# Layer 0 without GpSimd's wide elementwise work, and 24 modulation rows as float32 products on four 32-column strips

## The chip, the cores and the metric

One core of one Trainium2 chip runs the kernel. The metric is the device time of one execution in microseconds (us). The engines are TensorE (PE; its weight loads are shown as PEld), VectorE (DVE), ScalarE (ACT), GpSimd (POOL) and SyncE (SP), which issues the loads.

## The reference

A trunk of two layers over 256 tokens of width 1024, everything in float32. Each layer is a mixer and a gated ConvFFN, each behind an RMSNorm whose scale, shift and gate come from a conditioning vector `c`:

```python
c_act = jax.nn.silu(c)
for layer in range(DEPTH):
    mod = c_act @ ada_w[layer] + ada_b[layer]          # 1024 x 6144 weights
    sh1, sc1, g1, sh2, sc2, g2 = jnp.split(mod, 6, axis=-1)
    hmix = rmsnorm(x, norm_mix[layer]) * (1.0 + sc1) + sh1
    y = hgrn2_mixer(hmix, ...) if layer == 0 else nsa_mixer(hmix, ...)
    x = x + g1 * y
    hffn = rmsnorm(x, norm_ffn[layer]) * (1.0 + sc2) + sh2
    x = x + g2 * conv_ffn(hffn, ...)
return rmsnorm(x, final_norm)
```

HGRN2, the mixer of layer 0, is a gated linear recurrence with 8 heads of 128. It projects `hmix` to queries q, forget gates f, inputs i and output gates g, runs the recurrence, norms each head, multiplies by silu(g) and projects back to the width of the trunk.

## The kernel before, in words

Activations lie feature-major: 8 chunks of 128 features on the partitions, 256 tokens along the row. A matrix product is made of three float32r products: both the weights and the activations are split into a high and a low part (`whi`, `wlo`, `XH`, `XL`), and high x high, high x low and low x high are added up in PSUM (`mm3`).

All weights come through one stream (class `Stream`). A unit is 128 x 1024 values (512 KB), loaded by SP into one of seven `raw` buffers. A unit of weights is then split: ACT casts `whi` (L106), and DVE, or in some units POOL, subtracts it to get `wlo` (L113), into one of five split buffers. `use(k)` is called where TensorE takes unit k. It splits ahead up to unit k + 3, so whatever a split issues stands in program order ahead of the products of unit k. SP and PE run in the order of the program; DVE, ACT and POOL are ordered by Tile's priorities, except in the opening, which is written out by hand.

Among the units of weights lie 96 rows of the modulation (function `ada`): a unit holds 128 features of one row, one per partition, and one DVE instruction multiplies it by silu(c), broadcast to all partitions in `cb`, and sums along the row into a column of `mod` (L244). In layer 0 some rows go another way: POOL multiplies (L241), and ACT sums in a second pass over the row (L242).

Layer 0 has these stages, by the profile's clock:

- **The opening** (to about 75 us, `opening`): eight chunks of the normed residual, each with two rows of the modulation (the even one on POOL) and two units of weights, `hg_a`. DVE's order per chunk is: row, the columns `gs_t` and `sh_t` of the next chunk, `xn`, `XL`, `wlo`, (row,) `wlo`. PE's order per chunk is eight products each of (`XH`, `whi`), (`XL`, `whi`), (`XH`, `wlo`) at L379, then twelve 512 wide ones at L484. In chunks 2 to 5 the second `wlo` is halved between DVE and POOL (`U1`).
- **Preparing the first four heads** (to about 87 us): `prepare` makes queries, gates and keys; POOL scales the keys (L575) and subtracts three whole units (`HG_LOW`); PE starts the token-major products `hg_i2`.
- **The first chain** (to about 134 us): `diag`, five `level`s and three `blocks`, each a group of float32 products into a PSUM bank of the tag `aux` (which has two banks). After each, `grow` multiplies the queries `hqp` on DVE (L617) and the keys `hks` on POOL (L618). Between the steps of the chain PE does products of `hg_b` (`weave`).
- **The values of the first heads and the second chain** (to about 185 us): the same for heads 4 to 7, with products of `hg_g2` in between.
- **The tail of the mixer** (to about 209 us): values and turn of the second heads, the projection `hg_out`, and the residual (`finish_out`); then `ffn` begins with `mod_cols` and the norm.

From the third unit of `hg_b` to the last of `hg_out`, 18 units of weights have 24 rows among them (`mix`): 8 gates of the mixer and the 16 shift and scale rows of the ConvFFN. Before, every second of the 24 goes to POOL and ACT, the others to DVE.

## Time and profile before

| | us |
|---|---|
| median of 3 runs | 777.64 (776.15 to 781.36) |
| span of the profiled execution, first to last instruction | 774.9 |
| busy in that span: PE / DVE / ACT / POOL | 725.1 / 598.5 / 410.4 / 230.6 |
| mean granted clock of TensorE | 0.968 |
| loaded from memory | 158.48 MB, 206 GB/s over the span |

The profile gives no time of its own execution beside the span; the median lies 2.7 us above the span. A busy share is an average over stages with different limits, and a PE that shows as busy can still run at half clock or be held up by its weight loads. So stages have to be read one by one.

### The profile page before, as it was taken

The page shows a single profiled execution, that of the slowest core. Times are in us where ns is not written, and L with a number is a line of the kernel's source. Part 1 is how long each engine was busy: PE and PEld are TensorE (multiplying, and loading weights), DVE is VectorE, ACT ScalarE, POOL GpSimd, SP SyncE. Part 2 cuts the span into 40 slices and gives each one's busy share as a digit, 9 for nine tenths or more (in the row PEclk, how much of TensorE's full clock was granted, in tenths as well). Part 3 has the DMA queues.
Part 4 walks back from the last instruction along what each step waited for, and adds up shares of the span by engine and source line. Part 5 has one row for each costly group of instructions (what it writes and reads, how often), then busy time and mean ns, then how long its engine had stood idle before and what let it go on. Part 6 is the DMA issues. An engine that isn't in the chain of part 4 may idle for free.

```text
span 774.9 us, 14443 instructions
## 1 busy us (share of the span) xinstructions
PE 725.1 (94%) x5492; PEld 678.1 (88%) x5492; DVE 598.5 (77%) x1041; ACT 410.4 (53%) x756; POOL 230.6 (30%) x247
## 2 busy tenths in 40 slices
PE   7879888888999999999999999999999999999996
PEld 6767778768999999999989987756889999999995
DVE  5999987898599788778969877886768866666653
ACT  4456325426366444446545676776545744555544
POOL 4455647564203135111130015543520201101102
PEclk8999989999999999999999999987999999999998
DMA  8789655755368888899957960010237666776701
GB/s 302 269 274 313 204 191 191 268 192 193 110 219 300 297 280 270 294 267 341 344 191 254 355 207 21 35 56 1 85 134 271 196 217 214 215 221 210 209 18 55
DMA packets 48855, 160.45 MB, mean 207 GB/s; under 512 B 9362, under 2 KB 9618, under 8 KB 48787
## 3 DMA queue, kind: packets, MB, share of 16 engines
q1 hardware_dynamic: 48496, 159.02, 61.8%
q8 instruction: 43, 0.70, 0.4%
q10 hardware_dynamic: 290, 0.53, 0.2%
q14 instruction: 26, 0.20, 0.1%
HBM read 158.48 MB, written 1.05 MB: 206 GB/s over the span
## 4 chain that ended last, share of the span: by engine, by line
PE 72%; DVE 14%; issue 5%; POOL 5%; ACT 3%; DMA 2%; POOLq 0%; DVEq 0%; ACTq 0%
PE mm L316 10%; PE mm L318 10%; PE mm L317 10%; PE acc L379 9%; PE acc L317 7%; PE acc L316 7%; PE acc L318 7%; DVE wlo L113 4%; DVE raw L244 4%; PE acc L1006 2%; PE aux L1076 2%; PE aux L599 2%; POOL wlo L113 1%; PE acc L1005 1%; DMA raw<-ada 1%
## 5 line engine op out<-in xcount | busy, mean ns | idle before, releaser
L113 DVE TENSOR_TENSOR wlo<-raw,whi 128x1024 fp32r<-128x1024 f32 x193 | 247.1, 1291 | 66.8 <-ACT whi L106 66.5
L106 ACT CAST whi<-raw 128x1024 fp32r<-128x1024 f32 x201 | 207.9, 1047 | 138.2 <-PE acc L317 56.3
L316 PE MATMUL mm<-XH,whi 128*128 128x256 f32 x640 | 180.8, 283 | 1.0 <-DVE ff L791 0.9
L318 PE MATMUL mm<-XH,wlo 128*128 128x256 f32 x640 | 178.7, 279 | 0.0
L317 PE MATMUL mm<-XL,whi 128*128 128x256 f32 x640 | 178.4, 279 | 0.0
L796 POOL TENSOR_TENSOR fl<-ff,fh 128x256 fp32r<-128x256 f32 x44 | 43.9, 1002 | 302.9 <-ACT fh L794 297.8
L244 DVE SCALAR_TENSOR_TENSOR raw<-raw,cb 128x1024 f32<-128x1024 f32 x77 | 107.1, 1392 | 25.3 <-DMA raw<-ada 25.2
L316 PEld LDWEIGHTS mm<-XH,whi 128*128 128x128 f32 x640 | 119.9, 187 | 3.9 <-DVE ff L791 1.4
L318 PEld LDWEIGHTS mm<-XH,wlo 128*128 128x128 f32 x640 | 120.2, 188 | 0.0
L317 PEld LDWEIGHTS mm<-XL,whi 128*128 128x128 f32 x640 | 120.1, 188 | 0.0
L317 PE MATMUL acc<-fl,whi 128*128 128x256 f32 x352 | 98.5, 280 | 0.3 <-POOL fl L796 0.3
L316 PE MATMUL acc<-fh,whi 128*128 128x256 f32 x352 | 98.5, 280 | 0.0
L318 PE MATMUL acc<-fh,wlo 128*128 128x256 f32 x352 | 98.4, 280 | 0.0
L317 PEld LDWEIGHTS acc<-fl,whi 128*128 128x128 f32 x352 | 66.2, 188 | 0.5 <-POOL fl L796 0.5
L318 PEld LDWEIGHTS acc<-fh,wlo 128*128 128x128 f32 x352 | 66.2, 188 | 0.0
L316 PEld LDWEIGHTS acc<-fh,whi 128*128 128x128 f32 x352 | 66.1, 188 | 0.0
L241 POOL TENSOR_TENSOR raw<-raw,cb 128x1024 f32<-128x1024 f32 x19 | 49.4, 2599 | 14.2 <-DVE sh_t L414 9.2
L113 POOL TENSOR_TENSOR wlo<-raw,whi 128x1024 fp32r<-128x1024 f32 (+1 forms) x12 | 30.7, 2558 | 69.4 <-ACT whi L106 69.4
L379 PE MATMUL acc<-XH,whi 128*128 128x256 f32 x256 | 36.2, 283 | 8.8 <-ACT XH L398 8.0
L789 ACT ACTIVATE cv<-cv 128x256 f32<-128x256 f32 x44 | 18.0, 415 | 46.8 <-DVE cv L788 46.5
L379 PEld LDWEIGHTS acc<-XH,whi 128*128 128x128 f32 x256 | 32.5, 188 | 11.6 <-ACT XH L398 10.3
L1028 POOL TENSOR_SCALAR PR<-PR,rsum 128x128 f32<-128x128 f32 (+1 forms) x64 | 28.3, 463 | 43.3 <-DVE SC L1015 24.0
(221 smaller groups left out, 1456.4 us busy)
## 6 DMA issues: line engine op xcount, KB each, us to landing
raw<-ada SPq DMA_DIRECT2D x96, 512.0 KB, 4.9
raw<-up SPq DMA_DIRECT2D x88, 512.0 KB, 4.6
raw<-down SPq DMA_DIRECT2D x44, 512.0 KB, 4.5
raw<-hg_a SPq DMA_DIRECT2D x16, 512.0 KB, 5.9
raw<-hg_b SPq DMA_DIRECT2D x8, 512.0 KB, 5.8
raw<-hg_out SPq DMA_DIRECT2D x8, 512.0 KB, 4.5
raw<-nsa_a SPq DMA_DIRECT2D x8, 512.0 KB, 4.8
raw<-nsa_q SPq DMA_DIRECT2D x8, 512.0 KB, 4.9
```

The source lines that it names most:

```text
L106: self.nc.scalar.copy(hi, t)
L113: eng.tensor_sub(lo[:, c], t[:, c], hi[:, c].bitcast(FT))
L241: nc.gpsimd.tensor_mul(t, t, cb)
L244: nc.vector.scalar_tensor_tensor(t, t, 1.0, cb, op0=OP.mult, op1=OP.mult, accum_out=m)
L316: nc.tensor.matmul(o, wh, xh, start=start, stop=False, skip_group_check=True)
L317: nc.tensor.matmul(o, wh, xl, start=False, stop=False, skip_group_check=True)
L318: nc.tensor.matmul(o, wl, xh, start=False, stop=stop, skip_group_check=True)
L379: nc.tensor.matmul(half(accs, m), a[:, w], x[:, c], start=c == 0 and m % 2 == 0 and n == 0, stop=c == NC - 1 and n == 2, skip_group_check= ...
L599: nc.tensor.matmul(ps[:, (2 * h + t) * 64:(2 * h + t + 1) * 64], self.KS[:, h, x], q, start=True, stop=True)
L789: nc.scalar.activation(t, t, AF.Silu)
L796: return nc.gpsimd.tensor_sub(fl, f, fh.bitcast(FT))
L1028: nc.gpsimd.tensor_scalar(p, p, r[:, t, br:br + 1], 0.0, op0=OP.mult, op1=OP.add)
```

## The change

Seven rows of the opening, four halved `wlo` and three whole `wlo` move from POOL to DVE. The scaling of the keys (8 instructions) and their growth (28) move from POOL to DVE. What POOL keeps in layer 0 is small: the `pow` of the norms, the adds of squares and some fills.

The 24 rows between the third unit of `hg_b` and the end of `hg_out` are no longer sums on DVE, POOL and ACT. Their weights come transposed (`ada_k`), again 24 units of 512 KB: a pair of units holds two rows' 2 x 128 features as columns, and 8 chunks of the contraction, four per unit. When the second unit of a pair is split, PE multiplies all eight chunks in float32: the stationary operand is a chunk of silu(c), repeated over 32 columns (`cs`), the moving one 256 columns of weights. The four chunks of a unit go to four strips of 32 output partitions, and the second unit adds to the same strips. ACT copies the 128 x 256 result to SBUF (`sums`); one step of the stream later (`turned`) PE adds up the four strips and turns them onto the partitions with two products against a column `quarter`, and DVE copies two columns to `mod`. `mix` gives the unit of the first row of a pair the first half and that of the second the other, so the rows' places in the stream stay. The last pair is turned at the start of `ffn`, ahead of `mod_cols`. Silu of `c` for `cs` is computed in the opening ahead of the squares of the norm.

```diff
@@ -106,11 +104,7 @@
         def rest():
-            parts = low if isinstance(low, tuple) else (low,)
-            w = D // len(parts)
-            for n, eng in enumerate(parts):
-                c = slice(n * w, (n + 1) * w)
-                eng.tensor_sub(lo[:, c], t[:, c], hi[:, c].bitcast(FT))
+            low.tensor_sub(lo, t, hi.bitcast(FT))
...
@@ -223,6 +217,12 @@
+    ccol = consts.tile([P, NC], FT, name="ccol")
+    cs = consts.tile([P, NC, 32], FT, name="cs")
+    quarter = consts.tile([P, 1], FT, name="quarter")
+    nc.gpsimd.memset(quarter, 0.0)
+    for j in range(4):
+        nc.gpsimd.memset(quarter[32 * j:32 * j + 1], 1.0)
...
+    held, turning = [], []
+
+    def turned():
+        while turning:
+            turning.pop(0)()
+
+    def ada_pair(n, half):
+        def then(t):
+            held.append(t)
+            if not half:
+                return turned()
+            tiles = [held.pop(0) for _ in range(2)]
+            turned()
+            ps = bank("aux")
+            for u, x in enumerate(tiles):
+                for j in range(4):
+                    nc.tensor.matmul(ps[32 * j:32 * j + 32, :S], cs[:, 4 * u + j], x[:, j * S:(j + 1) * S],
+                                     start=u == 0, stop=u == 1, skip_group_check=True)
+            sums = work.tile([P, S], FT, name="sums")
+            nc.scalar.copy(sums, ps[:, :S])
+
+            def turn():
+                for k in range(2):
+                    nc.tensor.matmul(ps[:, S + k:S + k + 1], sums[:, k * P:(k + 1) * P], quarter, start=True, stop=True,
+                                     skip_group_check=True)
+                nc.vector.tensor_copy(mod[:, n:n + 2], ps[:, S:S + 2])
+
+            turning.append(turn)
+        return st.add(I["ada_k"][:, (n - 16) // 2, half], then)
...
@@ -270,13 +301,13 @@
         if c + 1 < NC:
-            ada(2 * c + 2, pool=True)
-        u_a[c].append(st.add(I["hg_a"][:, c, 1], low=(nc.vector, nc.gpsimd) if c in U1 else None))
+            ada(2 * c + 2)
+        u_a[c].append(st.add(I["hg_a"][:, c, 1]))
...
-    ids = mix(ws[:HG_LATE], [], low=HG_LOW) + mix(ws[HG_LATE:], ada_units(0, "g1") + ada_units(0, "2"), range(0, 24, HG_POOL))
+    ids = mix(ws[:HG_LATE], []) + mix(ws[HG_LATE:], ada_units(0, "g1") + ada_units(0, "2"), pairs_=True)
...
@@ -517,6 +548,8 @@
         lower_bound()
+        nc.scalar.activation(ccol, part("c"), AF.Silu)
+        nc.vector.tensor_copy(cs, ccol[:, :, None].to_broadcast([P, NC, 32]))
         norm = Norm(7, nc.vector)
...
@@ -572,7 +605,7 @@
-                nc.gpsimd.tensor_scalar(self.KS[:, h], self.KS[:, h], a, 0.0, op0=OP.mult, op1=OP.add)
+                nc.vector.tensor_scalar(self.KS[:, h], self.KS[:, h], a, None, op0=OP.mult)
...
@@ -615,7 +648,7 @@
-                    nc.gpsimd.tensor_mul(k[:, hs], k[:, hs], T[:, hs, :, 1:2].to_broadcast([P, 2, n // 2, m]))
+                    nc.vector.tensor_mul(k[:, hs], k[:, hs], T[:, hs, :, 1:2].to_broadcast([P, 2, n // 2, m]))
...
@@ -759,6 +792,7 @@
     weave((critical(B.chain()), HG_WEAVE[0]), (one_after_another(first_of(g2, HG_TURN), A.turn(), g2, *outs[:HG_OUT[0]]), HG_WEAVE[1]))
+    turned()
     gate_cols(0)
...
         first, units = u_f[layer]
+        turned()
         mod_cols(k, nffn, 0, NC)
```

## Rows read from the trace of the kernel before

**Rows 1.** Windows: stages of layer 0; length, busy us per engine (instructions), PE clock, DMA, GB/s

```profile
47.80:55.80 8.00, 5.89 (x36) 4.99 (x36) 7.41 (x8) 3.42 (x6) 4.59 (x2) 1.00 0.81 256
63.80:69.60 5.80, 5.76 (x37) 5.20 (x38) 5.16 (x10) 3.99 (x6) 0.00 (x0) 1.00 0.82 270
...
87.20:134.20 47.00, 40.14 (x327) 38.92 (x328) 37.43 (x56) 16.59 (x26) 28.73 (x21) 0.89 0.60 201
134.20:184.85 50.65, 42.46 (x282) 36.74 (x281) 46.26 (x70) 22.68 (x51) 30.52 (x23) 0.90 0.63 212
184.85:208.90 24.05, 24.05 (x206) 24.05 (x205) 15.62 (x30) 12.44 (x32) 5.46 (x7) 1.00 0.56 190
```

**Rows 2.** Timeline, chunk 4 of the opening: start, length, engine, line, tiles [idle before]

```profile
48.21 2.93 DVE L113 TENSOR_TENSOR wlo<-raw,whi 128x1024 fp32r<-128x1024 f32 x2
...
50.55 2.84 POOL L241 TENSOR_TENSOR raw<-raw,cb 128x1024 f32<-128x1024 f32 x1
...
51.06 3.41 DVE L244 SCALAR_TENSOR_TENSOR raw<-raw,cb 128x1024 f32<-128x1024 f32 x1
```

**Rows 3.** Timeline, chunk 1 of the opening, where POOL has nothing to do

```profile
22.52 1.21 DVE L244 SCALAR_TENSOR_TENSOR raw<-raw,cb 128x1024 f32<-128x1024 f32 x1
...
25.49 2.35 DVE L113 TENSOR_TENSOR wlo<-raw,whi 128x1024 fp32r<-128x1024 f32 x2
...
27.76 1.22 DVE L244 SCALAR_TENSOR_TENSOR raw<-raw,cb 128x1024 f32<-128x1024 f32 x1
```

**Rows 4.** Timeline, first products of chunks 1, 4 and 7

```profile
25.36 1.10 PE L379 MATMUL acc<-XH,whi 128*128 128x256 f32 x8
...
47.83 1.21 PE L379 MATMUL acc<-XH,whi 128*128 128x256 f32 x8 [2.24 <-ACT XH L398]
...
69.58 1.10 PE L379 MATMUL acc<-XH,whi 128*128 128x256 f32 x8
```

**Rows 5.** Timeline, from the opening to the first chain

```profile
75.54 0.47 PE L316 MATMUL mm<-whi,XH 128*128 128x512 f32 x1 [0.17 <-DVE V L742]
...
76.03 5.79 POOL L113 TENSOR_TENSOR wlo<-raw,whi 128x1024 fp32r<-128x1024 f32 x2
...
81.85 1.95 PE L585 MATMUL aux<-hq,hks 128*128 128x128 f32 x16
...
87.20 0.39 PE L318 MATMUL acc<-XH,wlo 128*128 128x256 f32 x1 [3.16 <-DVE wlo L113]
```

**Rows 6.** Groups by line and shape, 18 to 209 us: xcount | busy us, mean ns

```profile
L617 DVE TENSOR_TENSOR hqp<-hqp,ht 128x256 f32<-128x256 f32 x28 | 25.8, 947 | 2.3 <-PE aux L599 1.9 <-PE aux L641 0.3
...
L618 POOL TENSOR_TENSOR hks<-hks,ht 128x256 f32<-128x256 f32 x28 | 26.8, 970 | 35.5 <-PE aux L599 25.8 <-issue 5.2 <-DVE OL L701 1.8
```

**Rows 7.** Timeline, levels of both chains: DVE with nothing of POOL's in the way

```profile
104.77 0.77 DVE L605 COPY_PREDICATED hst<-masks,aux 128x256 f32<-128x256 uint32 x2
...
161.33 0.78 DVE L617 TENSOR_TENSOR hqp<-hqp,ht 128x256 f32<-128x256 f32 x2
```

**Rows 8.** Timeline, float32 products, each two passes; and the product behind the third

```profile
7.06 1.98 PE L516 MATMUL mm<-cb,ones 1*128 1x512 f32 x4
...
119.61 0.70 PE L630 MATMUL aux<-hqp,hks 128*32 128x32 f32 x32
120.24 0.39 PE L316 MATMUL acc<-XH,whi 128*128 128x256 f32 x1
...
134.19 1.05 PE L669 MATMUL aux<-V,hst 128*128 128x128 f32 x8
```

**Rows 9.** Windows: the clock around the first two of these (columns as in rows 1)

```profile
7.06:9.00 1.94, 1.94 (x6) 0.69 (x5) 1.33 (x4) 1.75 (x4) 0.00 (x0) 1.00 1.00 357
...
119.60:120.20 0.60, 0.60 (x33) 0.59 (x32) 0.60 (x2) 0.60 (x1) 0.60 (x2) 1.00 0.75 239
```

**Rows 10.** Waits of PE, 75 to 209 us: us in total, times, longest

```profile
PE aux L599 <- DVE hqp L617: 6.6, 5, 2.3
```

**Rows 11.** Timeline, DVE where the ConvFFN's norm begins

```profile
210.65 0.16 DVE L325 TENSOR_SCALAR msq<-aux 128x2 f32<-128x2 f32 x1 [1.43 <-PE aux L361]
```

More of the change, by code (lines that the diff above doesn't have):

```diff
@@ L39 @@
 TSOON = 75
-U1 = range(2, 6)
 HG_LATE = 6
 FFN_LATE = 8
-HG_POOL = 2
-HG_LOW = (0, 1, 2)
 NSA_LOW = (6, 8)
@@ L62 @@
 SMALL = {}
-for _n, _w in (("ada_b", 96), ("norm_mix", 16), ("norm_ffn", 16), ("final_norm", 8), ("hg_lb", 16), ("hg_gnorm", 1)):
+for _n, _w in (("ada_b", 96), ("norm_mix", 16), ("norm_ffn", 16), ("final_norm", 8), ("hg_lb", 16), ("hg_gnorm", 1),
+               ("c", 8)):
     SMALL[_n] = (sum(w for _, w in SMALL.values()), _w)
@@ L234, in trunk, with ada @@
     st = Stream(nc, raws, splits, *LOOK)
-    def ada(n, pool=False):
+    def ada(n):
         def then(t):
-            m = mod[:, n:n + 1]
-            if pool:
-                nc.gpsimd.tensor_mul(t, t, cb)
-                return lambda: nc.scalar.activation(t, t, AF.Copy, accum_out=m)
-            else:
-                nc.vector.scalar_tensor_tensor(t, t, 1.0, cb, op0=OP.mult, op1=OP.mult, accum_out=m)
-        return st.add(I["ada"][:, n], then)
+            nc.vector.scalar_tensor_tensor(t, t, 1.0, cb, op0=OP.mult, op1=OP.mult, accum_out=mod[:, n:n + 1])
+        return st.add(I["ada"][:, n], then)
+    held, turning = [], []
[23 more added lines that the diff above has]
+        return st.add(I["ada_k"][:, (n - 16) // 2, half], then)
     def ada_units(layer, which):
@@ L251, in ada_units, with mix @@
         return list(range(b + a, b + e))
-    def mix(ws, adas_, pool=(), low=()):
+    def mix(ws, adas_, low=(), pairs_=False):
         ids, n, m = [], len(ws), len(adas_)
@@ L259, in mix @@
             while done < m and done * n < (k + 1) * m:
-                ada(adas_[done], done in pool)
+                if pairs_:
+                    ada_pair(adas_[done - done % 2], done % 2)
+                else:
+                    ada(adas_[done])
                 done += 1
@@ L1183, in _layout @@
     a["ada"] = order(f["ada_w"].transpose(0, 2, 1))
-    small = {"ada_b": order(f["ada_b"])}
+    a["ada_k"] = a["ada"][:, 16:40].reshape(P, 12, 2, 2, 4, P).transpose(5, 1, 3, 4, 2, 0).reshape(P, 12, 2, D)
+    small = {"ada_b": order(f["ada_b"]), "c": f["c"].reshape(NC, P).T}
     for n in ("norm_mix", "norm_ffn"):
```

## The prediction

> **What bounds the kernel now.** I read the page first (PE busy in 94% of the span), then windows by stage, because only layer 0 is touched. Behind it, from 209 us on, nothing of the change runs, so the whole difference must arise ahead of it. The windows [rows 1] show three kinds of stage. In a chunk of the opening PE is busy 5.89 of 8.00 us while DVE shows 7.41 and POOL 4.59. In the two chains PE shows 40.14 of 47.00 and 42.46 of 50.65, but at a mean clock of 0.89 and 0.90: there PE waits, cools down and then works at half speed. In the tail of the mixer PE is busy 24.05 of 24.05 us at full clock: nothing is idle there.
>
> Next the timeline of a chunk [rows 2], to see why DVE is so full. A row of the modulation takes 1.21 us on DVE where POOL has nothing to do [rows 3], but 3.41 beside POOL's product of 2.84, and ends right with it (50.55 + 2.84 = 53.39; 51.06 + 3.41 = 54.47, one undisturbed row behind). Two `wlo` take 2.35 undisturbed [rows 3] and 2.93 beside POOL [rows 2]. So DVE does not share with POOL, it stands still. The same shows in the chains: L617 takes 0.39 alone [rows 7] and 0.95 in the mean [rows 6]. Every microsecond of POOL's wide work costs DVE nearly one. The waits of PE then name DVE: 6.6 us on `hqp` alone [rows 10], and 3.16 at the end of the preparation, where POOL's two `wlo` of 5.79 had held up DVE [rows 5].
>
> The Trainium skill, SBUF — State Buffer, section "SBUF: two separate sides", calls the ports that these two engines share an exclusive lock. The trace agrees (1.21 against 3.41).
>
> **The change part by part.**
>
> *Opening, chunks 1 to 7.* Undisturbed, the period with one row on DVE is 27.76 - 22.52 = 5.24 us [rows 3]. The second row adds 1.21 and its accumulator read, so I take 6.5 for chunks 1 to 6; the halved `wlo` is already whole in that period. The last period is undisturbed today and stays 5.8 [rows 1]. From chunk 1 to 7: 5 x 6.5 + 5.8 = 38.3 against 69.58 - 25.36 = 44.2 [rows 4], **-6**. DVE is still the bound (PE needs 5.89 [rows 1]). The loads must bring 2.1 MB in 6.5 us, 323 GB/s, between the 256 of today's chunk [rows 1] and the 357 seen at the start [rows 9]. Ahead of chunk 1, the blocked row there gets its 1.3 us back, and silu of `c` with its table switch now stands ahead of the squares on ACT and costs about as much: nothing.
>
> *Preparing the first heads.* From chunk 7's first product to the product that waited is 87.20 - 69.58 = 17.6 us. PE's own work in it is the chunk (5.9), the steps of `hg_i2` (75.54 to 81.85, 6.3) and `diag` (1.95) [rows 5]: 14.2. DVE gets three more `wlo`, four key scalings, and still has three `wlo`, four copies of 512, four scalings and the products: 6 x 1.18 + 4 x 0.77 + 8 x 0.39 + 1.2 + 0.8 = 15.3, some of it behind PE's last step. I take 14.1 to 15.3 with little of DVE's excess showing: **-3.5** (-2 to -3.5).
>
> *A pair on TensorE.* Four float32 passes of 512 columns took 1.98 [rows 8] at full clock [rows 9]: 0.45 a pass with little tail, so 0.22 for 256 columns. Eight products are 16 passes: 3.5 us one after the other, 1.1 if four strips run at a time. The only row with strips is L630: 32 passes of 32 columns, alternating between two strips, from 119.61 to 120.24 [rows 8], 20 ns each, where 32 columns at the above rate give 28. So strips do overlap, 1.4 times with the group's entry and exit in it, which gives 2.5 us. In the new order the two passes of one product write the same strip and stand one behind the other, so the next strip's first pass can run beside the second at best: overlap by two, (8 + 1) x 0.22 = 2.0. I take 2.0; the ends are 1.1 and 3.5. The turn is four passes that load 128 columns, at 1.05 / 8 = 0.13 [rows 8]: 0.5. So **2.5 a pair**, 30 us for twelve, put on the engine that is the bound.
>
> The Trainium skill, TensorE: Matmul & The Clock Gate, Part 3, says that products on different column strips run at once and gives 2.38 for three strips, but also that products start strictly in program order. By its ratio a pair would be 3.5 / 2.38 + 0.5 = 2.0 and the sum 6 us lower; by its order the two passes of a strip hold up the next one, which is my 2.0 for the products alone.
>
> *Where the pairs fall.* Splitting runs three units ahead, so four pairs are issued in the first chain's stage, four in the second's, four in the tail. They stand ahead of the unit's products in PE's queue: if the second unit's load, a bank of `aux` or (for the turn) ACT's copy is late, all products behind wait, and with them the chain. Loads run about seven units ahead, over 10 us of PE's time, and ACT loses twelve sums over 1024 columns; I cost these waits at nothing but for one: in the tail a turn stands directly between two pairs (ahead of `finish_out`), and the copy costs some 0.6.
>
> *First chain.* With the lost clock taken off (11% of 47.0 is 5.2), PE's work is 40.14 - 5.2 = 34.9; with four pairs 45. DVE per step: two copies 0.77, L617 0.78 [rows 7], and now the keys, the same again: 2.3 and the handovers, against some 2.2 of other products between two steps (the weave's 21.0 to 16.4). Steps with a pair between don't wait, the others about 0.5, more where DVE is in a `wlo`: 2.5. So 47.4, **+0.5**. The 12 DVE rows that go (1.21 each) more than pay for 28 key products at 0.39.
>
> *Second chain.* 42.46 - 5.1 = 37.4, and 10 is 47.4. Here only 1.6 us lie between two steps (15.5 to 16.4), so four steps wait 1 us, and the values' norm 1: 52.4, **+2**.
>
> *Tail.* PE has nothing idle [rows 1], so four pairs show in full: 4 x 2.0 + 3 x 0.5 + 0.6 = **+10**. The last turn and DVE's copy fall where DVE is idle 1.43 us for the norm [rows 11], so they cost nothing; without that cover, 0.6.
>
> Sum: -6 - 3.5 + 0.5 + 2 + 10 = +3. On the span that is 774.9 + 3 = 777.9; the median lies 2.7 above the span, so 777.64 + 3 = **780.6 us**. What DVE gains, PE spends.
>
> **The rivals.**
>
> - *Four strips at a time.* A pair is 1.6 instead of 2.5: 12 x 0.9 = 11 less, of which the chains give back about 1.5 as waits that pairs no longer cover: 771. For it: L630's strips overlap. Against it: two passes per product in order.
> - *Strips one after the other* (the rival on the slow side). Pairs cost 4.0: 18 more, of which waits in the chains absorb 3: 796. It decides from 2.6 us per pair on, where the sum leaves 1%. For it: no row has four strips; L630's passes are short. Against it: 20 ns instead of 28.
> - *The opening doesn't get faster*, since the loads, not DVE, set its pace: at the 256 GB/s of today 2.1 MB take 8.2 us, and the -6 is gone: 786.6. Against it: 357 GB/s [rows 9].
> - *DVE becomes the chains' bound*: the keys wait behind a `wlo` of 1.18 in most of 15 steps, which were on POOL before: some 10 more, 790. Against it: 0.95 falls to 0.39 in L617.
>
> **How the numbers follow.** Forecast 0.45 (alone: 772 to 788, from the ends of the opening and the waits), four strips 0.2, one after the other 0.15, no faster opening 0.1, DVE 0.1. Measured differences under 1% (770 to 785.4) can't be told from no change. Faster by over 1%: half of four strips and a sixth of the forecast, with a little for an opening that gives more: 0.2. Slower: nearly all of strips one after the other and DVE, half of the opening's rival, a sixth of the forecast: 0.35. Within 1%: 0.45. The range goes from below the four strips to the serial case: 765 to 797.
>
> **What would show it.** In the profile after: first products of chunks 6.5 us apart; rows in the opening at 1.2 and L617 at 0.39; the stage between chunk 7 and the chain under 15 us; a pair's 16 passes start to end 2.0 (1.1 and 3.5 decide for the rivals); the stage from the values of the second heads to the residual 34 us instead of 24. Wrong would make it a pair far from 2.0, loads that PE waits for ahead of a pair, or PE's clock at 0.5 in the chains again.

## The result, and the profile after

The changed kernel takes 784.5 us (median of 20 runs, 779.4 to 790.5) against 777.9 us in the same session: a ratio of 1.0083, with a 95% interval of 1.0062 to 1.0105. The profiled execution spans 783.0 us, 8.1 more than the 774.9 before. So it is about 6.6 us slower, just inside the 1% that the prediction called the same; 780.6 had been forecast.

Lines of the changed kernel in what follows: L239 a row on DVE, L107 `wlo`, L410 the opening's first products, L775 the copies of `V`'s first half, L618 `diag`, L632/L663/L674/L681 the chain's steps, L650 and L651 the growth of queries and keys (L617 and L618 before), L702 the heads' values, L729 and L734 their transposes and `OL`, L261 a pair's products, L264 ACT's copy of the sums, L268 the turn. Beside them stand L91 the loads, L104 ACT's cast, L347 to L349 the three products of `mm3`, L515 the opening's 512 wide products, L609 the queries' preparation and L714 the norm of the values (`hO`).

The windows by stage come first: from chunk 7's first products to the first product beside the chain, first chain, second chain, tail. They are cut at the same events as [rows 1] but for one: there the first chain is counted from the third product beside it, the one that waited, which begins at 84.42 here. So 0.3 us of the first chain would belong to the stage before it. The columns are stretch, length, busy us of PE, PE's weight loads, DVE, ACT and POOL, PE clock, DMA share, GB/s.

```profile
62.08:84.10 22.02, 15.74 (x77) 13.17 (x77) 17.01 (x26) 13.40 (x16) 0.00 (x0) 0.84 0.77 253
84.10:124.66 40.56, 40.56 (x412) 37.72 (x411) 28.71 (x65) 13.05 (x21) 0.00 (x0) 1.00 0.61 203
124.66:175.50 50.84, 45.62 (x362) 37.66 (x361) 32.28 (x75) 19.00 (x44) 2.02 (x1) 0.97 0.50 157
175.50:215.80 40.30, 33.10 (x284) 29.34 (x284) 14.15 (x28) 12.94 (x34) 5.35 (x6) 0.92 0.56 182
```

Against [rows 1] the first chain is 6.4 us shorter, with PE busy in all of it; the second has its old length; the tail is 40.3 us instead of 24.05, and PE is idle in 7.2 of it. The first of the four stages is 22.0 us long instead of 87.20 - 69.58 = 17.6 [rows 4, 5]. That stage and the tail are where the gain went.

**The opening** did as forecast. Timeline of PE at chunks 1, 6 and 7, and of DVE in chunk 2:

```profile
24.57 1.10 PE L410 MATMUL acc<-XH,whi 128*128 128x256 f32 x8
...
55.68 1.21 PE L410 MATMUL acc<-XH,whi 128*128 128x256 f32 x8 [0.49 <-ACT XH L429]
62.08 1.21 PE L410 MATMUL acc<-XH,whi 128*128 128x256 f32 x8 [0.51 <-ACT XH L429]
```

```profile
31.62 1.22 DVE L239 SCALAR_TENSOR_TENSOR raw<-raw,cb 128x1024 f32<-128x1024 f32 x1
...
32.76 1.22 DVE L107 TENSOR_TENSOR wlo<-raw,whi 128x1024 fp32r<-128x1024 f32 x1
```

From chunk 3 on chunks are 6.40 us apart, a row takes 1.22 instead of 3.41 [rows 2], and chunk 7 begins at 62.08 instead of 69.58 [rows 4]: 7.5 us won.

**What took them back** stands in PE's waits between 62 and 216 us (engine, tile and line, what it waited for; us in total, times, longest):

```profile
PE mm L347 <- DVE V L775: 6.3, 1, 6.3
PE aux L729 <- DVE OL L734: 3.4, 2, 1.8
PE aux L261 <- DVE OL L734: 3.1, 1, 3.1
PE aux L261 <- DVE hO L714: 1.7, 1, 1.7
PE aux L663 <- DVE OL L734: 1.6, 1, 1.6
```

The wait for `hqp` of [rows 10], 6.6 us, is gone. The first row is new. The timelines of DVE and of PE around it:

```profile
69.41 1.22 DVE L609 TENSOR_TENSOR hqp<-hq,ht 128x1024 f32<-128x1024 f32 x1
70.55 1.22 DVE L107 TENSOR_TENSOR wlo<-raw,whi 128x1024 fp32r<-128x1024 f32 x1
...
72.28 1.22 DVE L107 TENSOR_TENSOR wlo<-raw,whi 128x1024 fp32r<-128x1024 f32 x1
73.42 1.28 DVE L775 COPY V<-mm 128x512 f32<-128x512 f32 x2
```

```profile
66.88 0.63 PE L515 MATMUL mm<-wlo,XH 128*128 128x512 f32 x2
...
74.25 0.76 PE L347 MATMUL mm<-whi,XH 128*128 128x512 f32 x1 [6.27 <-DVE V L775]
74.81 0.63 PE L348 MATMUL mm<-wlo,XH 128*128 128x512 f32 x1
75.24 0.63 PE L349 MATMUL mm<-whi,XL 128*128 128x512 f32 x1
```

The bank is complete at 67.5, but the two copies that empty it stand behind the whole preparation and two `wlo` in DVE's order. `hg_i2`'s products wait 6.27 us, and the first twelve then follow each other at 0.43 us instead of 0.23, at half clock (windows of these and of the stretch in the tail that comes below, columns as above):

```profile
74.25:79.51 5.26, 5.26 (x13) 4.09 (x14) 3.06 (x4) 0.00 (x0) 0.00 (x0) 0.50 0.85 247
193.13:199.01 5.88, 5.88 (x35) 4.61 (x36) 0.01 (x1) 0.37 (x1) 0.00 (x0) 0.50 0.84 254
```

`diag` begins at 82.40, where it began at 81.85 before [rows 5]: 20.3 us behind chunk 7 instead of 12.3.

**A pair** takes 1.07 us from its first pass to its last, not 2.0, and the turn 0.50. Timeline of PE:

```profile
88.88 1.07 PE L261 MATMUL aux<-raw,cs 128*32 128x256 f32 x16
...
175.15 0.50 PE L268 MATMUL aux<-quarter,sums 128*128 128x1 f32 x4
```

**The tail**, in one timeline over SyncE's queue, PE, ACT and DVE:

```profile
182.91 1.07 PE L261 MATMUL aux<-raw,cs 128*32 128x256 f32 x16 [1.66 <-DVE hO L714]
...
184.04 1.33 SPq L91 DMA_DIRECT2D raw<-hg_out  x1
...
189.00 0.66 PE L729 MATMUL aux<-ident,hO 128*128 128x128 f32 x4 [1.56 <-DVE OL L734]
...
190.12 1.04 ACT L104 CAST whi<-raw 128x1024 fp32r<-128x1024 f32 x1 [1.96 <-DMA raw<-hg_out]
...
191.07 0.68 ACT L733 ACTIVATE OH<-aux,small 128x512 fp32r<-128x512 f32 x1
...
192.33 0.74 DVE L734 SCALAR_TENSOR_TENSOR OL<-aux,small,OH 128x512 fp32r<-128x512 f32 x1
...
193.13 1.93 PE L261 MATMUL aux<-raw,cs 128*32 128x256 f32 x16 [3.14 <-DVE OL L734]
...
195.38 0.42 PE L348 MATMUL acc<-OL,whi 128*128 128x256 f32 x1
195.59 0.41 PE L349 MATMUL acc<-OH,wlo 128*128 128x256 f32 x1
```

Read it downwards. There are two `aux` banks. The pair of 182.91 waits for a bank that the values hold, and with it wait the load buffers that it has to free: the load of `hg_out` goes out at 184.04, right behind it. The pair's bank stays taken until its turn is copied to `mod`, so the second two transposes find one bank for two jobs and wait for `OL` (189.00). ACT, in order, first waits for the late load, casts, and only then copies `OH`; `OL` is late by that, and the next pair waits 3.14 us for a bank. TensorE has by then been mostly idle for 6 us (1.00 us busy from 187.44 to 193.13) and runs at half clock (0.50), 0.21 us a product instead of 0.12, until 199.

The last turn is hidden under the norm, as forecast. Behind layer 0 little changed: 567.2 us from 215.80 on, 566.0 from 208.90 before. The norm's first step, `msq`, comes at 217.27 instead of 210.65 [rows 11], and that is most of the difference of the spans, 6.6 of 8.1 us.

### The profile page after: what moved, and what is told of

Same layout as the page of the kernel before. It is cut to its first block, busy times and chain, and to the rows that moved or that the text cites. A ratio compares the mean times of both kernels' runs of the same rounds, so it can differ in the third digit from the quotient of the medians.

```text
span 783.0 us, 14806 instructions
## 1 busy us (share of the span) xinstructions
PE 739.1 (94%) x5732; PEld 684.0 (87%) x5732; DVE 565.5 (72%) x1083; ACT 395.6 (51%) x731; POOL 134.4 (17%) x190
## 2 busy tenths in 40 slices
DMA packets 48856, 160.49 MB, mean 205 GB/s; under 512 B 9361, under 2 KB 9617, under 8 KB 48786
## 4 chain that ended last, share of the span: by engine, by line
PE 71%; DVE 13%; issue 5%; DMA 5%; ACT 3%; POOL 3%; DVEq 0%; POOLq 0%; ACTq 0%
PE mm L347 10%; PE mm L349 9%; PE mm L348 9%; PE acc L410 8%; PE acc L347 6%; PE acc L348 6%; PE acc L349 6%; DVE wlo L107 4%; DMA raw<-ada 4%; DVE raw L239 4%; PE aux L632 2%; PE aux L1111 2%; PE acc L1041 2%; PE aux L261 2%; PE acc L1040 1%
## 5 line engine op out<-in xcount | busy, mean ns | idle before, releaser
L107 DVE TENSOR_TENSOR wlo<-raw,whi 128x1024 fp32r<-128x1024 f32 x196 | 244.3, 1253 | 76.0 <-ACT whi L104 75.6
L104 ACT CAST whi<-raw 128x1024 fp32r<-128x1024 f32 x201 | 208.0, 1047 | 151.6 <-PE acc L348 60.1
L347 PE MATMUL mm<-XH,whi 128*128 128x256 f32 x640 | 180.6, 282 | 1.1 <-DVE ff L826 1.1
L349 PE MATMUL mm<-XH,wlo 128*128 128x256 f32 x640 | 178.4, 279 | 0.0
L347 PEld LDWEIGHTS mm<-XH,whi 128*128 128x128 f32 x640 | 119.9, 187 | 3.9 <-DVE ff L826 1.5
L349 PEld LDWEIGHTS mm<-XH,wlo 128*128 128x128 f32 x640 | 120.2, 188 | 0.0
L239 DVE SCALAR_TENSOR_TENSOR raw<-raw,cb 128x1024 f32<-128x1024 f32 x72 | 92.1, 1281 | 23.4 <-DMA raw<-ada 23.3
L347 PE MATMUL acc<-fh,whi 128*128 128x256 f32 x352 | 98.5, 280 | 0.0
L349 PE MATMUL acc<-fh,wlo 128*128 128x256 f32 x352 | 98.4, 280 | 0.0
L349 PEld LDWEIGHTS acc<-fh,wlo 128*128 128x128 f32 x352 | 66.2, 188 | 0.0
L347 PEld LDWEIGHTS acc<-fh,whi 128*128 128x128 f32 x352 | 66.1, 188 | 0.0
L410 PE MATMUL acc<-XH,whi 128*128 128x256 f32 x256 | 36.0, 282 | 4.5 <-ACT XH L429 4.5
L357 POOL TENSOR_TENSOR rst<-msq,mhalf 128x2 f32<-128x2 f32 (+1 forms) x7 | 8.2, 1168 | 180.0 <-DVE msq L356 180.0
L410 PEld LDWEIGHTS acc<-XH,whi 128*128 128x128 f32 x256 | 32.2, 188 | 7.5 <-ACT XH L429 7.4
L429 ACT ACTIVATE XH<-xn,sh_t 128x256 fp32r<-128x256 f32 x32 | 15.3, 503 | 43.1 <-DVE xn L428 43.0
L829 ACT CAST fh<-ff 128x256 fp32r<-128x256 f32 x44 | 17.5, 405 | 37.9 <-DVE ff L826 37.8
```

Source lines behind the costliest of these rows:

```text
L104: self.nc.scalar.copy(hi, t)
L107: low.tensor_sub(lo, t, hi.bitcast(FT))
L239: nc.vector.scalar_tensor_tensor(t, t, 1.0, cb, op0=OP.mult, op1=OP.mult, accum_out=mod[:, n:n + 1])
L347: nc.tensor.matmul(o, wh, xh, start=start, stop=False, skip_group_check=True)
L349: nc.tensor.matmul(o, wl, xh, start=False, stop=stop, skip_group_check=True)
L410: nc.tensor.matmul(half(accs, m), a[:, w], x[:, c], start=c == 0 and m % 2 == 0 and n == 0, stop=c == NC - 1 and n == 2, skip_group_check= ...
```

## The experiments

Twelve kernels were run, each timed beside the kernel before. The table shows where each one's profiled execution stood: the start of chunk 7's first products, of `diag`, of the first and the second heads' values, and of the norm's `msq`, all in us. For the run with a bank of its own alone no stages are listed; they are read from the run with both edits.

| kernel | chunk 7 | `diag` | values 1 | values 2 | `msq` | ratio to before (95%) |
|---|---|---|---|---|---|---|
| before | 69.58 | 81.85 | 134.19 | 184.87 | 210.65 | 1 |
| after | 62.08 | 82.40 | 124.66 | 175.52 | 217.27 | 1.0083 (1.0062 to 1.0105) |
| e1_v_first | 62.15 | 76.01 | 118.27 | 169.14 | 210.78 | 1.0011 (0.9975 to 1.0048) |
| e2_own_bank | | | | | | 0.9959 (0.9929 to 0.9990) |
| e3_both | 62.27 | 76.12 | 118.38 | 165.32 | 200.90 | 0.9878 (0.9844 to 0.9911) |
| e4_one_strip | 61.68 | 81.81 | 135.42 | 197.64 | 249.00 | 1.0491 (1.0442 to 1.0540) |
| e5_rows | 62.35 | 82.82 | 119.35 | 160.95 | 190.16 | 0.9734 (0.9666 to 0.9802) |
| e6_pairs | 71.52 | 85.69 | 127.94 | 178.46 | 219.63 | 1.0103 (1.0058 to 1.0148) |
| e7_front | 61.97 | 75.83 | 121.19 | 168.59 | 203.47 | 0.9870 (0.9835 to 0.9904) |
| e8_rows_v | 62.27 | 76.14 | 117.53 | 160.49 | 189.66 | 0.9728 (0.9668 to 0.9787) |
| e9_opening | 62.20 | 82.42 | 120.68 | 161.40 | 187.95 | 0.9661 (0.9593 to 0.9729) |
| e10_chains | 70.41 | 90.82 | 127.82 | 172.23 | 200.74 | 0.9845 (0.9775 to 0.9915) |
| e11_best | 61.64 | 73.50 | 114.30 | 158.02 | 184.13 | 0.9653 (0.9608 to 0.9697) |
| e12_gp_rows | 62.11 | 82.25 | 128.38 | 178.87 | 204.42 | 0.9892 (0.9827 to 0.9958) |

### V's copies first

```diff
-    for t in range(2):
-        nc.vector.tensor_copy(V[t][:, :512], ips[t])
+    with soon():
+        for t in range(2):
+            nc.vector.tensor_copy(V[t][:, :512], ips[t])
```

> The changed kernel with one edit: the two copies of V's first half, which empty the banks that hg_i2's products wait for, are given the same urgency as the first heads' preparation and so stand ahead of its 12 VectorE instructions instead of behind them and behind two low parts. Theory 1 (the late copies cost 6.3 us of idle TensorE and some 2 us at half clock): TensorE's wait on V falls from 6.27 us to under 2, hg_i2's first product comes at 68 to 70 instead of 74.25, the second heads' products some 6 us earlier than 84.1, and the whole ends 5 to 8 us sooner, a ratio to the kernel before of 0.998 to 1.002 instead of 1.008. Rival (the stretch is bound by VectorE's work or by the loads whatever stands first): the wait moves behind the eighth step of hg_i2, to a low part or the diagonal products, the second heads' products still begin at 83 to 84, and the ratio stays at 1.007 to 1.010.

```profile
67.38 1.29 DVE L776 COPY V<-mm 128x512 f32<-128x512 f32 x2 [0.16 <-PE mm L515]
```

The copies now come at 67.38 (73.42 after), the wait for `V` is down to 0.2 us, `diag` begins 6.4 us sooner, and everything behind it is shifted by 6.4 to 6.5 us up to `msq`; the ratio falls by 0.7%. Theory 1 holds. What is left of the rival is one wait of 1.9 us for a `wlo`.

### A bank of its own for the turn

```diff
             def turn():
+                ps = bank("aux")
                 for k in range(2):
```

> The changed kernel with one edit: the turn of a pair's sums takes a bank of its own, so that the pair's bank comes free with ACT's copy, some 1 us behind the products, instead of with the copy to mod two units later. Theory 2 (in the second chain and behind it the short tiles' two banks are held by pairs not yet turned): TensorE's waits on OL, 1.83 and 1.56 us at the first heads' turn, 1.56 and 3.14 at the second heads', fall by half or more, and the mixer ends 3 to 6 us sooner, a ratio of 1.000 to 1.005. Rival (the banks are held by the transposes and the values themselves and by ACT, which comes late to them because its cast waits for a load): the waits on OL and hO stay, and the ratio stays at 1.006 to 1.011.

> Both edits: V's copies ahead of the first heads' preparation, and a bank of its own for the turn of a pair's sums. Theories 1 and 2 together: the gains add, since the one lies before 84 us and the other behind 125, 8 to 14 us, a ratio of 0.990 to 0.998. If only the first holds: 0.998 to 1.002. If neither: 1.006 to 1.011.

The ratio of the bank alone is 0.9959, that of both edits 0.9878: the bank is worth 1.2% from the changed kernel on and 1.3% from V's copies on, some 10 us where 3 to 6 had been expected. From e1 to e3 the second chain shrinks from 50.87 to 46.94 and the stretch behind it from 41.64 to 35.58. The waits themselves account for about half (those for `OL` fall by 5.1 us between e1 and e3); the clock brings the rest: PE is busy 4.8 us less with the same products. Windows of e1's second chain and of the stretch behind it up to `msq`:

```profile
118.27:169.14 50.87, 45.64 (x363) 37.70 (x361) 32.32 (x75) 18.93 (x44) 2.02 (x1) 0.97 0.47 158
169.14:210.78 41.64, 34.67 (x298) 30.91 (x297) 14.19 (x29) 13.34 (x35) 5.33 (x6) 0.92 0.52 174
```

In the run with both edits (windows: first chain, second chain, tail up to the last add to the residual; up to `msq` PE is busy 31.94 of 35.58 us):

```profile
76.12:118.38 42.26, 42.26 (x425) 39.42 (x424) 31.79 (x70) 14.09 (x22) 0.00 (x0) 1.00 0.70 238
118.38:165.32 46.94, 43.54 (x362) 36.78 (x361) 31.95 (x75) 18.47 (x44) 2.01 (x1) 1.00 0.52 172
165.32:198.98 33.66, 30.02 (x280) 26.95 (x280) 13.79 (x27) 12.92 (x34) 5.33 (x6) 1.00 0.64 215
```

The clock is 1.00 in all three, against 0.97 and 0.92 in the second chain and the tail of e1 and of the changed kernel. So both theories hold, and their gains add: 0.7 and 1.2% alone, 2.1% together. With both mends the change would have been 1.2% faster than the kernel before.

### All eight products of a pair on one strip

```diff
-                    nc.tensor.matmul(ps[32 * j:32 * j + 32, :S], cs[:, 4 * u + j], x[:, j * S:(j + 1) * S],
-                                     start=u == 0, stop=u == 1, skip_group_check=True)
+                    nc.tensor.matmul(ps[:32, :S], cs[:, 4 * u + j], x[:, j * S:(j + 1) * S],
+                                     start=4 * u + j == 0, stop=4 * u + j == 7, skip_group_check=True)
...
```

The lines left out make ACT's copy and the turn work on those 32 rows alone.

> The changed kernel with the eight products of a pair all on the first strip of 32 columns, accumulated there, and the turn over those 32 rows alone. Same passes, same loads, same sums. Theory (four strips work at the same time, 16 passes in 1.07 us): on one strip the passes follow each other at the rate of the 256-column passes of the projections, 0.22 us for one, so 16 take 3.5 us instead of 1.07; twelve pairs cost up to 29 us more, less what of it falls into TensorE's waits (some 10 us lie in the second chain and the tail): 15 to 29 us, a ratio of 1.028 to 1.046. Rival (the pairs lie in waits anyway, and the passes' rate does not matter): under 8 us, a ratio below 1.018. If the strips brought nothing, 16 passes would take 1.07 us here too and the time would be that of the changed kernel.

The same sixteen passes, timeline of PE:

```profile
88.30 3.64 PE L261 MATMUL aux<-raw,cs 128*32 128x256 f32 x16
```

3.64 us against 1.07 is a factor of 3.4 from four strips. Twelve times the difference is 31 us; the ratio rises by 4.1%, 32 us, a little over the upper end expected. None of it is hidden: from `diag` on the three stages of the table are 11.4, 11.4 and 9.6 us longer than after, for 10.3 us more in the four pairs of each. So a pair's price shows in full, wherever it stands.

### Each part alone

With the rows on VectorE, GpSimd out (no pairs):

```diff
-    ids = mix(ws[:HG_LATE], []) + mix(ws[HG_LATE:], ada_units(0, "g1") + ada_units(0, "2"), pairs_=True)
+    ids = mix(ws[:HG_LATE], []) + mix(ws[HG_LATE:], ada_units(0, "g1") + ada_units(0, "2"))
```

> One part alone: GpSimd stays out of the first layer's wide work as in the changed kernel, but the 24 rows are multiplied and summed by VectorE, 1.22 us each, as the opening's are; no pairs, no turns. Theory (VectorE has room, as its 28.7 busy us of 40.6 in the first chain of the changed kernel and 32.3 of 50.8 in the second say): TensorE loses 12 pairs of 1.57 us and the waits that they cause for banks, VectorE gains 29 us of work spread over 130, and the mixer's end (217.3 us in the changed kernel by the norm's first step) comes at 188 to 200, a ratio of 0.97 to 0.985: then the pairs were not worth their place. Rival (with rows in the queue, low parts and the chains' products are late as in the kernel before, and VectorE is the first chain's bound, 28.7 + 10 x 1.22 = 40.9 us of 40.6): the end comes at 205 to 215, a ratio of 0.99 to 1.005, and TensorE waits for hqp or wlo in both chains.

With the pairs, and GpSimd's wide work as in the kernel before (the edits of the two helpers that this needs are left out):

```diff
...
-            ada(2 * c + 2)
+            ada(2 * c + 2, pool=True)
...
-        u_a[c].append(st.add(I["hg_a"][:, c, 1]))
+        u_a[c].append(st.add(I["hg_a"][:, c, 1], low=(nc.vector, nc.gpsimd) if c in range(2, 6) else None))
...
-    ids = mix(ws[:HG_LATE], []) + mix(ws[HG_LATE:], ada_units(0, "g1") + ada_units(0, "2"), pairs_=True)
+    ids = mix(ws[:HG_LATE], [], low=(0, 1, 2)) + mix(ws[HG_LATE:], ada_units(0, "g1") + ada_units(0, "2"), pairs_=True)
...
-                nc.vector.tensor_scalar(self.KS[:, h], self.KS[:, h], a, None, op0=OP.mult)
+                nc.gpsimd.tensor_scalar(self.KS[:, h], self.KS[:, h], a, 0.0, op0=OP.mult, op1=OP.add)
...
-                    nc.vector.tensor_mul(k[:, hs], k[:, hs], T[:, hs, :, 1:2].to_broadcast([P, 2, n // 2, m]))
+                    nc.gpsimd.tensor_mul(k[:, hs], k[:, hs], T[:, hs, :, 1:2].to_broadcast([P, 2, n // 2, m]))
```

> The other part alone: the 24 rows are pairs on TensorE as in the changed kernel, but GpSimd has its wide work of the kernel before (seven of the opening's rows, half of four low parts, three low parts behind the opening, the keys' products and their preparation). Theory (VectorE and GpSimd slow each other down where both work, 1.22 us against 3.41 for a row): the opening keeps its 7.5 us, chunk 7 at 69 to 70 us, V's copies stand where the order puts them, the chains' waits for hqp are back in part, since each keys' product on GpSimd stretches the queries' beside it: the mixer's end at 217 to 225 us, a ratio of 1.008 to 1.018. Rival (the rows were what loaded VectorE and GpSimd; without them the chains are bound by TensorE's products, as in the changed kernel, whoever does the keys): the end at 210 to 217, 0.998 to 1.008, chains of 41 to 43 us and 48 to 51.

This pair of runs decides the case. The first part alone makes the kernel 2.7% faster, the second alone 1.0% slower. In e5 the 24 rows cost DVE 1.22 us each and still the chains take 36.5 and 41.6 us, against 52.3 and 50.7 before. Windows of its two chains:

```profile
82.82:119.35 36.53, 36.48 (x345) 35.91 (x344) 32.68 (x72) 12.61 (x18) 0.00 (x0) 1.00 0.56 187
119.35:160.95 41.60, 38.25 (x283) 32.95 (x282) 38.34 (x88) 15.96 (x38) 1.75 (x1) 1.00 0.55 173
```

DVE is busy 32.7 and 38.3 us: it had the room, and PE's 36.5 is what the prediction worked out as its work without pairs, 34.9, with the 1.95 of `diag`, at which these windows begin. In e6 the total came where the theory put it, but not for its reason: the chains are 42.25 and 50.5 us, the rival's numbers and those of the changed kernel (42.26 and 50.9). Keys on POOL cost the chains nothing there; the loss lies ahead of `diag` (85.69 against 82.40).

### The pairs ahead of the last projections

```diff
-    ids = mix(ws[:HG_LATE], []) + mix(ws[HG_LATE:], ada_units(0, "g1") + ada_units(0, "2"), pairs_=True)
+    ids = mix(ws[:HG_LATE], []) + mix(ws[HG_LATE:20], ada_units(0, "g1") + ada_units(0, "2"), pairs_=True) + mix(ws[20:], [])
```

on top of both mends.

> Both mends of the run before (V's copies first, a bank of its own for the turn) and one more: the twelve pairs are spread over the 14 weight units that end before the last four heads' projections, not over 18, so that none stands in the last projections. Theory 3 (in the tail the loads stand behind the pairs that hold their buffers, 34 us of waits of the load queue in 12 waits, and ACT's casts and the last heads' turn behind the loads): the stretch from the second heads' values to the end, 31.4 us with both mends, falls to 26 to 28, of which 4 pairs of 1.6 us only move into the second chain, so that the whole gains 1 to 4 us, a ratio of 0.983 to 0.987 against 0.988. Rival (a pair costs its 1.57 us wherever it stands, and two of three units being pairs crowds the loads of the chain): no gain or a loss of up to 4 us, 0.987 to 0.993.

`msq` comes at 203.47 instead of 200.90, the ratio is that of e3: the rival, nothing to tell from no change. The load queue's waits on pairs don't fall either (38.0 us in 12 instead of 34.2 in 12). But the edit doesn't empty the tail: five, five and two pairs stand in the first chain, the second chain and the tail, instead of four in each. With one pair more the first chain takes 45.4 us instead of 42.3; with two fewer the tail takes 34.9 instead of 35.6, at a clock of 0.95 instead of 1.00. So what a tail without pairs would take isn't shown.

### V's copies first, with rows

> GpSimd out of the wide work, the 24 rows on VectorE, and V's copies ahead of the first heads' preparation; no pairs. If the late copies cost the rows' version what they cost the pairs' version, it ends 5 to 8 us before the run with the rows alone. By the theory that VectorE has room: a ratio of 0.962 to 0.978, below the 0.988 of the pairs with both mends. By the rival that VectorE then bounds the chains: 0.983 to 0.998, and the pairs are worth keeping.

The edit of e1 on e5. `diag` comes 6.7 us sooner, but the first chain grows from 36.5 to 41.4 and the second from 41.6 to 43.0; `msq` gains 0.5 us, and the ratio is the same. In the first chain DVE is busy 38.2 us instead of 32.7, and PE, which waited for nothing there in e5, waits four times for a `wlo`:

```profile
PE acc L349 <- DVE wlo L107: 4.0, 4, 1.8
```

So what V's late copies cost depends on what comes next: with pairs, PE is the bound and time won ahead of the chain stays; with rows, DVE has the same work to do and most of the 6 us are waited for later.

### Which of GpSimd's jobs made the chains long

Two runs that build on each other: e9 is e5 with the keys' products and their preparation back on GpSimd (the last two edits of e6),

```diff
-                nc.vector.tensor_scalar(self.KS[:, h], self.KS[:, h], a, None, op0=OP.mult)
+                nc.gpsimd.tensor_scalar(self.KS[:, h], self.KS[:, h], a, 0.0, op0=OP.mult, op1=OP.add)
...
-                    nc.vector.tensor_mul(k[:, hs], k[:, hs], T[:, hs, :, 1:2].to_broadcast([P, 2, n // 2, m]))
+                    nc.gpsimd.tensor_mul(k[:, hs], k[:, hs], T[:, hs, :, 1:2].to_broadcast([P, 2, n // 2, m]))
```

and e12 is e9 with every other one of the chains' 24 rows on GpSimd and ACT, as in the kernel before (the helper's part is left out):

```diff
...
-                    ada(adas_[done])
+                    ada(adas_[done], pool_ and done % 2 == 0)
```

> The 24 rows on VectorE as in the run with the rows alone, and GpSimd out of the opening only: in the chains it multiplies the keys again (28 products of two heads and their eight preparations), as in the kernel before, while VectorE multiplies the queries, the rows and the low parts. In the run with the rows alone the first chain (diagonal products to the heads' values) takes 36.5 us and the second 41.6, against 52.3 and 50.7 before. Theory (the keys on GpSimd beside VectorE's products are what made the chains long): the first chain goes back to 44 to 52 us, the second to 46 to 51, a ratio of 0.985 to 1.0. Rival (with pairs the keys on GpSimd cost the chains nothing, 42.25 and 50.5 us against 42.26 and 50.9; it was the rows and low parts on GpSimd): chains of 36 to 39 and 41 to 44 us, a ratio of 0.971 to 0.979.

> The run with GpSimd out of the opening only, but 12 of the chains' 24 rows are multiplied on GpSimd and summed by ACT again, as in the kernel before; so this is the kernel before with the opening's part of the change. Theory (the rows on GpSimd, 2.5 us each beside VectorE, are what stretched the chains: VectorE's products took 0.95 us instead of 0.54 there): the chains go from 38.3 and 40.7 us back to 46 to 53 and 47 to 52, the norm's first step to 203 to 213, a ratio of 0.986 to 1.002. Rival (what made the chains long before was their start, with low parts late from the opening): 38 to 42 and 41 to 44, a ratio of 0.966 to 0.975.

The keys are not it: e9's chains take 38.3 and 40.7 us, the rival's numbers, and its ratio of 0.966 can't be told from e5's 0.973. The rows are: with 12 of them back on GpSimd the chains take 46.1 and 50.5 us, and 2.3% are lost. Windows of the two chains, of e9 and then of e12:

```profile
82.42:120.68 38.26, 36.70 (x346) 36.11 (x345) 34.84 (x62) 12.63 (x18) 14.49 (x16) 1.00 0.66 211
120.68:161.40 40.72, 38.12 (x283) 33.19 (x282) 35.88 (x71) 16.91 (x39) 15.60 (x17) 1.00 0.56 192
```

```profile
82.25:128.38 46.13, 40.45 (x345) 39.21 (x344) 42.79 (x59) 19.03 (x30) 28.70 (x22) 0.93 0.64 216
128.38:178.87 50.49, 42.79 (x283) 36.40 (x282) 44.08 (x70) 22.47 (x49) 28.72 (x22) 0.90 0.59 202
```

Of the 17.6 us that the rows cost in the two chains, PE is idle in 9.2; the other 8.4 are the same products at a lower clock, 0.93 and 0.90 instead of 1.00. PE's waits there name DVE (`hqp`, `ht`, `hO`) and POOL's `hks`; ACT, which sums these rows, ends 0.6 us of them. Groups by line and shape in the chains (xcount | busy us, mean ns), e9 first, then e12, whose lines are three further down:

```profile
L651 POOL TENSOR_TENSOR hks<-hks,ht 128x256 f32<-128x256 f32 x28 | 25.3, 915 | 43.0 <-PE aux L632 26.0 <-issue 12.9 <-PE aux L663 2.6
...
L650 DVE TENSOR_TENSOR hqp<-hqp,ht 128x256 f32<-128x256 f32 x28 | 14.2, 536 | 1.2 <-PE aux L632 1.2
```

```profile
L240 POOL TENSOR_TENSOR raw<-raw,cb 128x1024 f32<-128x1024 f32 x11 | 29.0, 2640 | 16.5 <-PE acc L351 6.2 <-DMA raw<-ada 5.7 <-ACT whi L104 4.6
...
L654 POOL TENSOR_TENSOR hks<-hks,ht 128x256 f32<-128x256 f32 x28 | 25.4, 916 | 21.8 <-PE aux L635 17.2 <-PE aux L666 2.0 <-issue 1.5
```

```profile
L653 DVE TENSOR_TENSOR hqp<-hqp,ht 128x256 f32<-128x256 f32 x28 | 26.3, 968 | 0.8 <-PE aux L677 0.7
```

The keys take POOL 0.92 us in both. DVE's queries beside them take 0.54 without POOL's rows and 0.97 with them, as they took 0.95 before [rows 6]; in the changed kernel, with nothing on POOL, they take 0.43. One place of e12's timeline shows how the mean comes about: a row begins on POOL while DVE is in the first of two queries, and the two queries together take 2.92 us instead of some 0.8.

```profile
112.02 2.92 DVE L653 TENSOR_TENSOR hqp<-hqp,ht 128x256 f32<-128x256 f32 x2
...
112.04 2.62 POOL L240 TENSOR_TENSOR raw<-raw,cb 128x1024 f32<-128x1024 f32 x1
```

A product in the chain waits behind a POOL row of 2.6 us that has nothing to do with the chain; behind a product of keys it has less to wait for. The Trainium skill, SBUF — State Buffer, section "SBUF: two separate sides", calls the ports that the two engines share an exclusive lock, which one instruction holds for all its length; the row of 2.62 beside the 2.92 agrees.

### The opening as before, and V's copies first with the keys on GpSimd

e10 is e5 with the opening's rows and low parts as in the kernel before (the first three edits of e6).

> The 24 rows on VectorE and GpSimd out of the chains, but the opening as in the kernel before: seven rows, half of four low parts and the three low parts behind it on GpSimd. Theory (the opening's 7.5 us count, since everything behind it comes so much later): chunk 7's first products at 69 to 72 us instead of 62, the diagonal products at 85 to 90 instead of 82.8, a ratio of 0.977 to 0.985 against 0.973. Rival (the opening's gain is spent before the diagonal products, where V's late copies and the low parts set the time, 81.85 us before and 82.40 after the change): the diagonal products at 81 to 84 us, a ratio of 0.970 to 0.976.

With the opening as before, `diag` comes at 90.82 instead of 82.82 and `msq` at 200.74 instead of 190.16; the ratio rises by 1.1%. With rows on DVE, and V's copies late in both, the opening's part is worth what it wins.

e11 is e9 with V's copies first (the edit of e1).

> The rows on VectorE, GpSimd out of the opening and left with the keys in the chains, and V's copies ahead of the first heads' preparation. In the run with the rows alone V's copies first brought the diagonal products 6.7 us forward, and the first chain gave 4.9 of it back, VectorE being its bound there (32.7 busy us of 36.5) with low parts late five times. Theory (with the keys on GpSimd VectorE has the room, so that the 6 us stay): the first chain stays at 38 to 39 us, the norm's first step comes at 181 to 183 us instead of 187.95, a ratio of 0.957 to 0.962. Rival (the chain is bound by VectorE's queue here too, rows and low parts before the products): the first chain grows to 42 to 44 us, 186 to 189, a ratio of 0.964 to 0.972.

Between the two: the first chain grows by 2.5 us and the second by 3.0, `msq` comes 3.8 us sooner, and the ratio, 0.9653, is not to be told from 0.9661. Both versions beat the kernel before and the changed one; e11_best took 752.1 us against 778.9. What the first chain gives back begins with a `wlo` that PE waits for, while DVE is busy in 5.49 of 5.50 us; ACT's casts of that stretch are done by 74.9, so it is DVE's queue and not a load. Behind it the clock is 0.68 from 79 to 84.

```profile
77.77 0.38 PE L349 MATMUL acc<-XH,wlo 128*128 128x256 f32 x1 [2.08 <-DVE wlo L107]
...
73.50:79.00 5.50, 3.42 (x28) 3.21 (x27) 5.49 (x10) 1.41 (x2) 0.00 (x0) 0.98 0.64 204
```

## Why the prediction was right or wrong

The time was inside a wide range, and the difference under 1% was forecast. But the sum came near by luck: the stages miss by -1.5, +7.9, -6.9, -1.8 and +6.3 us, and these mostly cancel. Stage by stage, forecast and measured:

- **Opening: -6, measured -7.5.** The mechanism held: period 6.40 for 6.5, rows 1.22; in a chunk DVE is busy 5.8 us and idle 0.6 for ACT's `XH`. Neither PE nor DVE waits for a load; only ACT's casts do, 1.8 us in five. (The last period, left at 5.8, is 6.40 too; the first is 5.64.) From chunk 1 on it took 62.08 - 24.57 = 37.5 us for the 38.3 forecast; another 0.8 came ahead of chunk 1, which I had put at nothing.
- **Preparing the first heads: -3.5, measured +4.4** (22.0 for 17.6). This step failed. I had added DVE's work to 15.3 us and asked only whether it fits, with V's copies among it; I didn't ask in which order it stands, and that PE waits for just these two. In [rows 5] `hg_i2` waited 0.17 us for `V`, and I carried that over to a new order. e1 gives the price: 6.4 us, the wait and the half clock behind it. The 3.16 us that PE waited for a `wlo` behind `diag` did go, as I had meant.
- **A pair: 2.5 us, measured 1.07 + 0.50 = 1.57.** The rival of four strips at a time had it right. My step "the next strip's first pass can run beside the second at best" is wrong: on one strip the passes take 3.64 us, on four 1.07. The Trainium skill, TensorE: Matmul & The Clock Gate, Part 3, has products on different strips run at once; the runs agree, with 3.4 from four. The rival on the slow side had a slip: by my own prices (15 us for 1.5 more a pair) the sum leaves 1% at about 3.0 us a pair, not at 2.6.
- **First chain: +0.5, measured -6.4.** Four pairs at 0.93 less are 3.7, and the steps' waits, 2.5, did not come: PE was busy in all 40.56 us, and DVE in 28.71 of them. DVE was not the bound, so that rival falls.
- **Second chain: +2, measured +0.2.** Again 3.7 less for the pairs, but waits for banks (3.4 of the 5.2 idle us are for `OL`) took most of it.
- **Tail: +10, measured +16.3.** The pairs are 4 x 1.07 + 3 x 0.5 + 0.84 = 6.6. The waits of 1.66, 1.56 and 3.14, all for banks, the first for one that the values hold, are 6.4; the half clock from 193 to 199 is some 2.7 (0.9 in the pair, 19 products at 0.095 more). Together 15.7. The step that failed is "a bank of `aux` ... I cost these waits at nothing". A pair holds its bank until the next pair's first unit comes up, and is a third user of two banks.
- **The last turn: nothing**, right.

Sum by stages: -7.5 + 4.4 - 6.4 + 0.2 + 16.3 = +7.0 on +3 forecast. With a pair at its true price and no other fault the sum would have been the rival's 771; e3, which mends the two waits, is at 0.9878, or 768, though its stages are not those of the sum.

The larger miss is one of weighing. "What DVE gains, PE spends" was right as far as it went: but the prediction treated the two parts as one exchange. The runs split `msq`'s +6.6 us from before to after like this: GpSimd out of the opening, -6.2 (e12); the rows off GpSimd onto VectorE, -16.5 (e9); the keys off GpSimd, +2.2, not to be told from none (e5); the rows from VectorE to TensorE, +27.1, of which 16.4 go with both mends (e3). The parts hold in this order: from e5's side the opening is worth 10.6 us (e10), and in e12 its 7.5 us are not there at `diag` (82.25 for 81.85) but come in the first chain. Everything that the change was good for came from the first two. In [rows 6] I read 0.95 us for the queries and put it down to all of POOL's wide work, "every microsecond" of which "costs DVE nearly one". That step is wrong for the keys: in e9 25.3 us of them make the 28 queries longer by some 3 us (0.54 for 0.43). e9 and e12 show that it was the rows of L241.

What stays open: why DVE's order puts V's copies late in some of these kernels and not in the one before was not tried, and neither was what makes e11's second chain 3 us longer.

## What to carry to other kernels

Before work is moved onto the engine that bounds the kernel, try leaving it where it is with its disturbance removed: here 24 rows fitted on VectorE once GpSimd's long instructions were gone, and moving them cost 27 us at the mixer's end, 11 with both mends. A new user of a rotating buffer is to be costed by how long it holds it, and who is next in line, not by its own length alone; and when one stage is made faster, look at the order of the short instructions that hand banks over at its end.

## What was not expected of the hardware

Float32 products, which the trace shows as two passes each, overlap nearly fully on four 32-column strips of TensorE: sixteen passes of 256 columns in 1.07 us, 3.64 on one strip. And GpSimd's products of 256 columns (0.92 us each) beside VectorE cost it little, 0.54 us instead of 0.43 for the queries, while with its products of 1024 columns, 2.6 us each, the same instructions took 0.97. That it is the length of the other engine's single instruction that VectorE waits out is read from places like the one shown (2.92 us for two queries beside a row of 2.62); no run gave GpSimd the same busy time in shorter instructions, which was 14.5 and 15.6 us in e9's chains and 28.7 in each of e12's.
